# Places of the split weights in on-chip memory: level with the other operand, or 64 bytes beside it

## The chip, the cores and the metric

The kernel runs on one core of a Trainium2 chip. The metric is the device time of one execution in microseconds (us). Before the change the median of three runs is 2192.39 us (2190.46 to 2193.99).

## The reference

One decoder layer on x of 512 tokens by 2048 features, all float32. RMSNorm, a token mixer, an output projection and RMSNorm are added to the residual; then RMSNorm, a gated feed-forward part with a short convolution, and RMSNorm are added again. Cut to what matters here:

```python
h = rmsnorm(x, attn_pre_norm)
proj = h @ w_in                        # 2048 -> 6160 columns
# gated linear attention (4 heads) and differential attention (4 heads)
o = concat([o_a, o_b])                 # 512 x 2048
x = x + rmsnorm(o @ w_o, attn_post_norm)
h = rmsnorm(x, ffn_pre_norm)
up = h @ w_ffn_in                      # 2048 -> 2 x 5632
a, b = up[..., :D_FF], up[..., D_FF:]
a = conv_w[0]*a[t-2] + conv_w[1]*a[t-1] + conv_w[2]*a[t] + conv_b
f = (gelu(a) * b) @ w_ffn_out          # 5632 -> 2048
x = x + rmsnorm(f, ffn_post_norm)
```

## The kernel before, in words

**Splitting.** Every large product is made of three fast ones. A float32 matrix is split into a high part (rounded to the fast type, `F32R`) and a low part (what the rounding lost), and the kernel sums high x high, high x low and low x high. The activations are split once into `ah` and `al` (32 KB each per partition, laid out as 4 token tiles x 16 slices x 128 columns). The weights are split while they stream: `load` brings 128 x 1024 floats ("a granule") into a `raw` tile, and `granule` (lines 103 to 110) lets ScalarE write the high part `whi` (line 107) and VectorE (DVE) the low part `wlo` (line 108) into two tiles with the tag `split`. These come from the pool `wpool`, which has six of them, 4096 bytes each: three granules. A few granules use other pools (`sp1` in the mixer, `sp2` in the passage to the feed-forward part, `sp3` in the down stage), which add a granule or more of room.

**Two shapes of product.** TensorE holds 128 columns of one operand (stationary, loaded by a weight load) and moves columns of the other past it. `mm_n` (lines 157 to 163) holds activations and moves 512 columns of weights; `mm_t` (lines 135 to 145) holds weights and moves 512 columns of activations, or 256 where it is given two token tiles.

**Stages.** 1. The mixer: projections by `mm_n` and `mm_t`, with the attention heads cut into pieces that are run in between. Line 356 and 357 (`forget_gate`) are products with a stationary tile `gas` of 80 columns per step, 16 steps, and 512 moving columns of `ah` and `al`. 2. The output projection, `proj_n` over 4 chunks of 512 columns. For each token tile `evac_m` (lines 601 to 605) takes a finished bank: ScalarE squares it into a scratch tile with a sum, DVE multiplies it by the gain into `m`. 3. `to_ffn`, whose order is written out by hand on all engines: the last chunk, `evac` (the norm's sum, line 629, and its root on GpSimd), `residual` (633), `square` (638), `scale` (644), `turn` (transposes), and between them the first products of the feed-forward part on two token tiles at a time (256 columns). 4. The up stage: units of 512 columns of `w_ffn_in`, ten pairs of units. A unit multiplies 2 x 2 blocks by a scheme of seven products instead of eight; its moving operands are quarters of `ah` and `al` and sums of quarters (`s5`, `s2`, `s3`, `s7`), 256 columns each. `up_prods` (lines 883 to 893) issues for each granule 2 x 4 x 3 = 24 products. GpSimd's queue adds weight blocks to one another by accumulating DMAs (line 840). After each pair of units `token_sums` (lines 949 to 970) makes four sums for the next stage with the helper `add` (line 959 is its operation): `s5`, then `s2` from `s5`, `s7`, and `s3` from `s2`, each stored to memory by a DMA on SP's queue. 5. The down stage, the same scheme with 512 moving columns (lines 988 to 990), and a last group with the final norm.

Outside the stages written by hand a planner orders the instructions of each engine from a model of their times; the order is fixed before the run. Each engine works through its own queue in order. SP's queue issues the loads and stores.

**Places.** A pool gives its tiles out of one stretch of on-chip memory, one after the other, and pools follow each other in the order of the code. `ident` is declared 104 columns wider than used; with it, `ah`, `al` and everything behind it that matters here (`raw`, `split`, the sums of quarters) begin at multiples of 512 bytes. The three lines that make the tiles are:

```python
hi, lo = ((spare or wpool).tile([P, GR], F32R, name=v, tag="split") for v in ("whi", "wlo"))
act(hi, raw, AF.Copy)
tt(lo, raw, hi.bitcast(F32), ALU.subtract)
```

Of the kernel before, what the change touches and what calls it, by code (L numbers as in the profile page):

```python
# [9 lines left out]
F32 = mybir.dt.float32  # L10
F32R = mybir.dt.float32r
U8 = mybir.dt.uint8
AF = mybir.ActivationFunctionType
# [4 lines left out]
P = 128  # L18
# [12 lines left out]
GR = 1024  # L31
# [4 lines left out]
def hybrid_layer(ctx: ExitStack, tc: tile.TileContext, x, attn_pre_norm, w_in, w_alpha_up, b_alpha,  # L36
# [7 lines left out]
    w_f3 = w_ffn_in[0].rearrange("(k p) c -> p k c", p=P)  # L44
    w_y3 = w_ffn_out[0].rearrange("(k p) c -> p k c", p=P)

    def dma(o, i):
        return nc.sync.dma_start(out=o, in_=i)
# [3 lines left out]
    act = nc.scalar.activation  # L52
# [10 lines left out]
    wpool = ctx.enter_context(tc.tile_pool(name="w", bufs=6))  # L63
# [11 lines left out]
    def bank(pool=None):  # L75
        return (pool or psa).tile([P, 512], F32, name="bank", tag="bank")

    fill = []
    pace = [0.0, 0.0]

# [17 lines left out]
    def load(src, a):  # L98
        raw = wpool.tile([P, GR], F32, name="raw", tag="raw", bufs=4)
        dma(raw.rearrange("p (a b) -> p a b", a=a), src)  # L100
        return raw

    def granule(src, a, raw=None, spare=None):
        if raw is None:
            raw = load(src, a)
        hi, lo = ((spare or wpool).tile([P, GR], F32R, name=v, tag="split") for v in ("whi", "wlo"))
        act(hi, raw, AF.Copy)  # L107
        tt(lo, raw, hi.bitcast(F32), ALU.subtract)  # L108
        r = "p (a b) -> p a b"
        return hi.rearrange(r, a=a), lo.rearrange(r, a=a)  # L110

    def rsqrt_mean(ss, n, width=1):
        t = small.tile([P, width], F32, name="ms", tag="ms")
        nc.gpsimd.tensor_scalar(t, ss, 1.0 / n, EPS, ALU.mult, ALU.add)
        r = small.tile([P, width], F32, name="rs", tag="rs")
        nc.gpsimd.tensor_tensor(r, t, nhalf[:, :width], ALU.pow)
        return r
# [5 lines left out]
    def transpose_into_act(src, t, slot0, n):  # L123
        for g in range(0, n, 4):
            m = min(4, n - g)
            b = bank()
            for j in range(m):
                nc.tensor.transpose(b[:, j * P:(j + 1) * P], src[:, (g + j) * P:(g + j + 1) * P], ident)
            bv = b[:, :m * P].rearrange("p (k c) -> p k c", k=m)
            split(ah[:, t, slot0 + g:slot0 + g + m, :], al[:, t, slot0 + g:slot0 + g + m, :], bv)  # L130
# [45 lines left out]

    mixer = ExitStack()
    sp1 = mixer.enter_context(tc.tile_pool(name="sp1", bufs=2))
    mx1 = mixer.enter_context(tc.tile_pool(name="mx1", bufs=1))
    mx = mixer.enter_context(tc.tile_pool(name="mx", bufs=6))  # L180

    def big8(name):
        return mx.tile([P, 2048], F32, name=name, tag="big8", bufs=6)
# [7 lines left out]

    def first_half(c):
        gb = big8("gb")
        jb = mx.tile([P, 1024], F32, name="jb", tag="jb", bufs=1)
        xts = [big8("xt") for _ in range(NT)]
        H2 = [slice(1024 * i, 1024 * (i + 1)) for i in range(2)]
        H4 = [slice(512 * i, 512 * (i + 1)) for i in range(4)]
        rs, raws, w = {}, {}, {}
        banks = [bank(psm) for _ in range(NT)]
        col = C_GV + 512 * c  # L200

        def load_x(t):
            for i in range(2):
                dma(xts[t][:, H2[i]], x2[t * P:(t + 1) * P, H2[i]])

        def load_w(*gs):
            for g in gs:
                raws[g] = load(w_in3[:, 2 * g:2 * g + 2, col:col + 512], 2)

        def weights(g):  # L210
            w[g] = granule(None, 2, raws[g], spare=sp1 if g == 3 else None)

        def square(t):
            ss = small.tile([P, 2], F32, name="ss2", tag="ss2", bufs=4)
            for i in range(2):
                act(jb, xts[t][:, H2[i]], AF.Square, accum_out=ss[:, i:i + 1])
            sm = small.tile([P, 1], F32, name="ss", tag="ss")
            nc.gpsimd.tensor_tensor(sm, ss[:, 0:1], ss[:, 1:2], ALU.add)
            rs[t] = rsqrt_mean(sm, D)

        def scale(t, *ps):
            for i in ps:
                stt(xts[t][:, H4[i]], xts[t][:, H4[i]], rs[t], gb[:, H4[i]], ALU.mult, ALU.mult)

        def turn(t, *ps):
            for i in ps:
                transpose_into_act(xts[t][:, H4[i]], t, 4 * i, 4)

        def prods(t, *gs):
            for g in gs:  # L230
                mm_n(banks, t, g, w[g])

        load_x(0)
        bcast_row(gb[:, H2[0]], attn_pre_norm[0, H2[0]])
        load_w(0, 1, 2)
        load_x(1)
        load_w(3)
        load_x(2)
        load_x(3)
        bcast_row(gb[:, H2[1]], attn_pre_norm[0, H2[1]])  # L240
        square(0)
        scale(0, 0, 1)
        weights(0)
        turn(0, 0, 1)
        weights(1)
        weights(2)
        square(1)
        prods(0, 0, 1)
        scale(1, 0, 1)
        prods(0, 2)  # L250
        weights(3)
        turn(1, 0, 1)
        square(2)
        prods(0, 3)
        square(3)
        scale(2, 0, 1)
        prods(1, 0, 1, 2)
        turn(2, 0, 1)
        prods(1, 3)
        scale(3, 0, 1)  # L260
        prods(2, 0, 1)
        turn(3, 0, 1)
        scale(0, 2, 3)
        prods(2, 2)
        turn(0, 2, 3)
        scale(1, 2, 3)
        prods(2, 3)
        turn(1, 2, 3)
        scale(2, 2, 3)
        prods(3, 0, 1)  # L270
        turn(2, 2, 3)
        scale(3, 2, 3)
        prods(3, 2)
        turn(3, 2, 3)
        prods(3, 3)
        return banks
# [313 lines left out]
    x1d = [dram.tile([P, D], F32, name=f"x1d{t}") for t in range(NT)]  # L590
    wo = ExitStack()
    sp2 = wo.enter_context(tc.tile_pool(name="sp2", bufs=8, reuse_waits="tile"))
    wp = wo.enter_context(tc.tile_pool(name="wo", bufs=1, reuse_waits="tile"))
    m = [wp.tile([P, D], F32, name=f"m{t}") for t in range(NT)]
    g1 = wp.tile([P, D], F32, name="g1")
# [3 lines left out]
    ssm = [wp.tile([P, 4], F32, name=f"ssm{t}") for t in range(NT)]  # L599

    def evac_m(c, t, b):
        jk = wp.tile([P, 512], F32, name="jk5", tag="jk5", bufs=1)
        act(jk, b, AF.Square, accum_out=ssm[t][:, c:c + 1])
        sl = slice(512 * c, 512 * (c + 1))
        tt(m[t][:, sl], b, g1[:, sl], ALU.mult)

    order = [(s + 8) % 16 for s in range(KT)]
    for c in range(3):
# [4 lines left out]
    def to_ffn():  # L613
# [34 lines left out]
                transpose_into_act(xr[t][:, 512 * i:512 * (i + 1)], t, 4 * i, 4)  # L648

        def weights_f(d, c0, g, spare=None):  # L650
            d[g] = granule(w_f3[:, 4 * g:4 * g + 4, c0:c0 + 256], 4, spare=spare)

        for g in range(KT // 2):
            weights(g)
# [69 lines left out]
    fp = fa.enter_context(tc.tile_pool(name="fa", bufs=2, reuse_waits="tile"))  # L724
# [96 lines left out]
    turn = [0]  # L821
    ff = sp3 = None

    class Unit:
        def __init__(self, a, block, prods, chain, out):
            self.a, self.block, self.prods, self.chain, self.out = a, block, prods, chain, out
            self.banks = {}

        def run(self, seg, op, raws):
            c = seg[0]  # L830
            if seg[1] == "0":
                self.banks[c] = self.chain(c)
            for g in range(2):
                turn[0] += 1
                hl = granule(None, self.a, raws[g], spare=sp3 if sp3 and turn[0] % 4 == 0 else None)
                self.prods(self.banks[c], op, g, hl, seg[1] == "0")

        def more(self, raws, j):
# [110 lines left out]
    def token_sums(gi, u0, u1):  # L949
        c, i = (gi - 1) // 2, (gi - 1) % 2  # L950
        T = [slice(0, 256), slice(256, 512)]
        a11, a21, a12, a22 = u0[:, :, T[0]], u0[:, :, T[1]], u1[:, :, T[0]], u1[:, :, T[1]]

        def put(n, src):
            dma(sd[c][n][:, i, :].rearrange("p (n t) -> p n t", n=2), src)

        def add(n, x, y, op):
            t = fp.tile([P, 2, 256], F32, name=n, tag="sum", bufs=3)
            tt(t, x, y, op)
            put(n, t)  # L960
            return t

        put("a11", a11)
        put("a12", a12)
        put("a22", a22)
        s5 = add("s5", a21, a22, ALU.subtract)
        s2 = add("s2", s5, a11, ALU.subtract)
        add("s7", a11, a21, ALU.subtract)
        add("s3", s2, a12, ALU.add)


    place = {"a11": (0, 0), "s5": (1, 0), "s2": (0, 1), "s3": (1, 1), "s7": (2, 0), "a12": (3, 0), "a22": (2, 1)}
# [74 lines left out]
    sp3 = ctx.enter_context(tc.tile_pool(name="sp3", bufs=2, reuse_waits="tile"))  # L1047
# [104 lines left out]
    for q, at in enumerate(((3, 1), (0, 0))):  # L1152
        raw = ff.tile([P, GR], F32, name="st", tag="st", bufs=4)
        dma(raw, ud0[:, 2 * q:2 * q + 2, :].rearrange("p n t -> p (n t)"))
        hi, lo = (piece(v, *at) for v in (ah, al))
# [34 lines left out]
```

## Time and profile before

| what | number |
|---|---|
| median of three runs | 2192.39 us |
| profiled execution | 2189.37 us |
| its span, first to last instruction | 2187.7 us |
| mean granted TensorE clock | 0.996 |
| TensorE busy | 2152.3 us, 98% |
| VectorE busy | 1417.3 us, 65% |
| ScalarE busy | 901.2 us, 41% |
| GpSimd busy | 207.2 us, 9% |
| moved by DMA | 303.83 MB, 139 GB/s on the mean |

Busy times overlap, so they do not add up to the span. PE is TensorE's products, PEld its weight loads, which run beside the products. A row of the costliest groups gives line, engine, operation, out<-in with buffer numbers left out, shape and count, then busy time and the mean duration of one. A matmul's duration is longer than the distance to the next one, since products overlap in the array; distances are read from starts, or from a count in a stretch. A row of the timeline begins with the start and the duration in us. A row for one line gives the least, the median and the greatest duration in ns.

### The profile page before, as it was taken

What the parts mean: (1) busy time and instruction counts of PE and PEld (TensorE: products, weight loads), DVE (VectorE), ACT (ScalarE), POOL (GpSimd) and SP (SyncE); (2) the same over time, 40 slices, a digit from 0 to 9 for tenths busy, and PEclk for the clock granted to TensorE, in tenths of its full rate; (3) what the DMA queues carried; (4) which work ended last, traced back from release to release, by engine and by line L of the source; (5) the groups of instructions that cost most, each with busy time, mean ns of one, the idle gap of its engine ahead of it and who ended that gap; (6) DMA issues with size and microseconds to landing.
All of it is one profiled execution on the core that took longest, in us unless ns stands there. A gap on an engine that the chain in (4) does not pass through costs nothing.

```text
span 2187.7 us, 31874 instructions
## 1 busy us (share of the span) xinstructions
PE 2152.3 (98%) x13009; PEld 1921.1 (88%) x13009; DVE 1417.3 (65%) x1721; ACT 901.2 (41%) x1162; POOL 207.2 (9%) x245
## 2 busy tenths in 40 slices
PE   7999999999999999999999999999999999999997
PEld 6878888888888889899999999999999878888886
DVE  5345554444453246786786776776777777888987
ACT  4233332333342234353443444444444454544433
POOL 1000000000000000011111111011011011011101
PEclk9999999999999999999999999999999999999999
DMA  6322222222224344447657667567567677677663
GB/s 210 103 69 80 74 78 78 77 78 87 77 91 160 106 154 164 115 107 180 153 128 182 145 138 181 139 150 175 135 157 178 169 210 208 183 187 183 158 175 135
DMA packets 218471, 303.83 MB, mean 139 GB/s; under 512 B 11776, under 2 KB 155572, under 8 KB 216404
## 3 DMA queue, kind: packets, MB, share of 16 engines
q1 hardware_dynamic: 165204, 238.87, 32.5%
q0 software_dynamic: 53120, 62.92, 18.5%
q8 instruction: 102, 1.67, 0.3%
q14 instruction: 45, 0.37, 0.1%
HBM read 273.97 MB, written 27.79 MB: 138 GB/s over the span
## 4 chain that ended last, share of the span: by engine, by line
PE 78%; issue 15%; DVE 2%; DMA 2%; POOL 1%; ACT 1%; SPq 0%; POOLq 0%; DVEq 0%; ACTq 0%
PE bank L892 10%; PE bank L891 10%; PE bank L893 10%; PE bank L161 6%; PE bank L163 6%; PE bank L162 6%; PE bank L145 5%; PE bank L143 5%; PE bank L144 5%; PE bank L989 2%; PE bank L990 2%; PE bank L988 2%; PE bank L409 1%; PE bank L477 1%; PE bank L508 1%
## 5 line engine op out<-in xcount | busy, mean ns | idle before, releaser
L108 DVE TENSOR_TENSOR wlo<-raw,whi 128x1024 fp32r<-128x1024 f32 x332 | 404.1, 1221 | 376.8 <-ACT whi L107 366.1
L107 ACT ACTIVATE whi<-raw 128x1024 fp32r<-128x1024 f32 x332 | 350.3, 1059 | 661.7 <-PE bank L892 185.4
L107 ACT ACTIVATE whi<-rt 128x1024 fp32r<-128x1024 f32 x240 | 252.7, 1058 | 306.0 <-PE bank L892 200.3
L108 DVE TENSOR_TENSOR wlo<-rt,whi 128x1024 fp32r<-128x1024 f32 x240 | 292.6, 1221 | 117.4 <-ACT whi L107 113.7
L893 PE MATMUL bank<-ah,wlo 128*128 128x256 f32 x1280 | 362.2, 283 | 0.0
L892 PE MATMUL bank<-al,whi 128*128 128x256 f32 x1280 | 362.2, 283 | 0.0
L891 PE MATMUL bank<-ah,whi 128*128 128x256 f32 x1280 | 362.2, 283 | 0.0
L161 PE MATMUL bank<-whi,ah 128*128 128x512 f32 x640 | 252.7, 398 | 0.2 <-ACT ah L120 0.2
L162 PE MATMUL bank<-wlo,ah 128*128 128x512 f32 x640 | 251.4, 393 | 0.2 <-DVE wlo L108 0.2
L163 PE MATMUL bank<-whi,al 128*128 128x512 f32 x640 | 250.2, 393 | 0.0
L892 PEld LDWEIGHTS bank<-al,whi 128*128 128x128 f32 x1280 | 245.8, 192 | 0.1
L891 PEld LDWEIGHTS bank<-ah,whi 128*128 128x128 f32 x1280 | 245.8, 192 | 0.1
L893 PEld LDWEIGHTS bank<-ah,wlo 128*128 128x128 f32 x1280 | 245.8, 192 | 0.0
L989 PE MATMUL bank<-wlo,ah 128*128 128x512 f32 x560 | 219.8, 393 | 6.6 <-DVE wlo L108 6.6
L990 PE MATMUL bank<-whi,al 128*128 128x512 f32 x560 | 219.2, 392 | 0.0
L988 PE MATMUL bank<-whi,ah 128*128 128x512 f32 x560 | 214.6, 392 | 3.3 <-DVE acc L996 2.0
L143 PE MATMUL bank<-ah,whi 128*128 128x512 f32 (+1 forms) x576 | 214.6, 373 | 0.0
L144 PE MATMUL bank<-al,whi 128*128 128x512 f32 (+1 forms) x576 | 212.9, 370 | 0.0
L145 PE MATMUL bank<-ah,wlo 128*128 128x512 f32 (+1 forms) x576 | 212.5, 369 | 0.3 <-DVE wlo L108 0.3
L163 PEld LDWEIGHTS bank<-whi,al 128*128 128x128 f32 x640 | 120.7, 189 | 26.0 <-DVE al L121 0.3
L162 PEld LDWEIGHTS bank<-wlo,ah 128*128 128x128 f32 x640 | 120.8, 189 | 25.8 <-DVE wlo L108 1.1
L161 PEld LDWEIGHTS bank<-whi,ah 128*128 128x128 f32 x640 | 120.6, 189 | 24.7 <-ACT ah L120 0.6
(222 smaller groups left out, 3716.2 us busy)
## 6 DMA issues: line engine op xcount, KB each, us to landing
raw<-in_w_in_dram SPq DMA_DIRECT2D x96, 512.0 KB, 3.7
raw<-in_w_ffn_in_dram SPq DMA_DIRECT2D x96, 512.0 KB, 4.7
raw<-in_w_ffn_out_dram SPq DMA_DIRECT2D x48, 512.0 KB, 6.7
rt<-in_w_ffn_in_dram SPq DMA_DIRECT2D x40, 512.0 KB, 5.4
rt<-in_w_ffn_in_dram POOLq DMA_DIRECT2D x40, 512.0 KB, 5.9
raw<-in_w_ffn_in_dram POOLq DMA_DIRECT2D x40, 512.0 KB, 7.0
raw<-in_w_o_dram SPq DMA_DIRECT2D x32, 512.0 KB, 3.6
rt<-in_w_ffn_out_dram SPq DMA_DIRECT2D x20, 512.0 KB, 6.3
```

What stands on the lines that cost most here:

```text
L107: act(hi, raw, AF.Copy)
L108: tt(lo, raw, hi.bitcast(F32), ALU.subtract)
L143: mm(o, wh, ah[:, t0:t1, kk, :], start=st, stop=False)
L144: mm(o, wh, al[:, t0:t1, kk, :], start=False, stop=False)
L145: mm(o, wl, ah[:, t0:t1, kk, :], start=False, stop=sp)
L161: mm(banks[t], ah[:, t, s, :], w[0][:, k, :], start=st, stop=False)
L162: mm(banks[t], ah[:, t, s, :], w[1][:, k, :], start=False, stop=False)
L163: mm(banks[t], al[:, t, s, :], w[0][:, k, :], start=False, stop=sp)
L891: mm(o, wh, sh[:, :, kk, :], start=start and kk == 0 and n == 0, stop=False, **NOW)
L892: mm(o, wh, sl[:, :, kk, :], start=False, stop=False, **NOW)
L893: mm(o, wl, sh[:, :, kk, :], start=False, stop=kk == HK - 1, **NOW)
L989: mm(b[j], sh[:, o:o + P], w[1][:, q, :], start=False, stop=False, **NOW)
```

## The change

The split tiles become 1152 instead of 1024 floats long (4608 bytes, 9 x 512), and `granule` uses 1024 of them from an offset: 0 as a rule; 16 floats (64 bytes) or 112 floats (448 bytes, 64 below the next multiple of 512) where its caller gives a place of 64 or -64. `narrow_place` gives -64 and 64 in turns, one for each granule. The up stage's units and the passage's `weights_f` ask for it, the others do not. The pools `sp1` and `sp2` keep tiles of 1024 floats and no offset. To make room, the scratch tile `jb` of the first norm becomes a `big8` tile, `evac_m` squares in place in the bank after the multiplication instead of into a scratch tile before it, and the sums of `token_sums` get two buffers instead of three.

```diff
+    SHIFT = {0: 0, 64: 16, -64: 112}
+    small_pools = []
+    side = [64]
+
+    def narrow_place():
+        side[0] = -side[0]
+        return side[0]
...
-    def granule(src, a, raw=None, spare=None):
+    def granule(src, a, raw=None, spare=None, place=0):
         if raw is None:
             raw = load(src, a)
-        hi, lo = ((spare or wpool).tile([P, GR], F32R, name=v, tag="split") for v in ("whi", "wlo"))
+        if spare in small_pools:
+            hi, lo = (spare.tile([P, GR], F32R, name=v, tag="split") for v in ("whi", "wlo"))
+        else:
+            o = SHIFT[place]
+            hi, lo = ((spare or wpool).tile([P, GR + 128], F32R, name=v, tag="split")[:, o:o + GR]
+                      for v in ("whi", "wlo"))
         act(hi, raw, AF.Copy)
         tt(lo, raw, hi.bitcast(F32), ALU.subtract)
...
     sp1 = mixer.enter_context(tc.tile_pool(name="sp1", bufs=2))
+    small_pools.append(sp1)
...
-        jb = mx.tile([P, 1024], F32, name="jb", tag="jb", bufs=1)
+        jb = big8("jb")[:, :1024]
...
     sp2 = wo.enter_context(tc.tile_pool(name="sp2", bufs=8, reuse_waits="tile"))
+    small_pools.append(sp2)
...
     def evac_m(c, t, b):
-        jk = wp.tile([P, 512], F32, name="jk5", tag="jk5", bufs=1)
-        act(jk, b, AF.Square, accum_out=ssm[t][:, c:c + 1])
         sl = slice(512 * c, 512 * (c + 1))
         tt(m[t][:, sl], b, g1[:, sl], ALU.mult)
+        act(b, b, AF.Square, accum_out=ssm[t][:, c:c + 1])
...
         def weights_f(d, c0, g, spare=None):
-            d[g] = granule(w_f3[:, 4 * g:4 * g + 4, c0:c0 + 256], 4, spare=spare)
+            d[g] = granule(w_f3[:, 4 * g:4 * g + 4, c0:c0 + 256], 4, spare=spare, place=narrow_place())
...
         def __init__(self, a, block, prods, chain, out):
+            self.narrow = prods is up_prods
...
-                hl = granule(None, self.a, raws[g], spare=sp3 if sp3 and turn[0] % 4 == 0 else None)
+                hl = granule(None, self.a, raws[g], spare=sp3 if sp3 and turn[0] % 4 == 0 else None,
+                             place=narrow_place() if self.narrow else 0)
...
         def add(n, x, y, op):
-            t = fp.tile([P, 2, 256], F32, name=n, tag="sum", bufs=3)
+            t = fp.tile([P, 2, 256], F32, name=n, tag="sum", bufs=2)
             tt(t, x, y, op)
```

## The prediction

> **What bounds the kernel now.** I read the page's busy times and costliest groups first, then the stretches, then who waits for whom in the longest stage, then single lines and rows.
>
> ```profile
> PE 2152.3 (98%) x13009; PEld 1921.1 (88%) x13009; DVE 1417.3 (65%) x1721; ACT 901.2 (41%) x1162; POOL 207.2 (9%) x245
> ```
> ```profile
> 720.00:800.00 80.00, 80.00 (x354) 66.24 (x354) 27.12 (x26) 24.04 (x34) 0.00 (x0) 1.00 0.31 107
> 930.00:1090.00 160.00, 160.00 (x1335) 160.00 (x1334) 117.48 (x118) 75.11 (x82) 20.51 (x16) 1.00 0.62 145
> ```
> ```profile
> ACT whi L107 <- PE bank L892: 384.4, 248, 2.1
> DVE u L919 <- PE bank L893: 18.3, 20, 0.9
> ```
>
> The stretch 930 to 1090 us lies in the up stage of the feed-forward part (line 891 to 893, 256 columns move). TensorE takes all of it, at granted clock 1.00, and 160.00 us / 1335 = 119.9 ns: one product starts each 120 ns. The second fence is the list of waits from 930 to 1725 us. No wait of TensorE is in it; ScalarE waits 384.4 us in 248 pieces for TensorE to free a split tile. DVE is busy 117.48 / 160 = 73%, the DMA engines 62%. So the pace of this stage is the distance between two products and nothing else. Where 512 columns move (720 to 800 us), the distance is 80.00 / 354 = 226 ns, with TensorE again full.
>
> ```profile
> L891 PEld LDWEIGHTS bank<-ah,whi x1280: 187/192/192, 927.1 to 1738.7; 128*128 128x128 f32 x183
> L891 PE MATMUL bank<-ah,whi x1280: 277/283/283, 927.3 to 1738.8; 128*128 128x256 f32 x183
> L891 PE MATMUL bank<-s5h,whi x320: 283/283/283, 933.0 to 1704.5; 128*128 128x256 f32 x160
> L891 PE MATMUL bank<-s2h,whi x320: 283/283/283, 936.2 to 1710.3; 128*128 128x256 f32 x160
> L891 PE MATMUL bank<-s3h,whi x320: 283/283/283, 941.9 to 1716.3; 128*128 128x256 f32 x160
> ```
>
> Line 891 issues 1280 + 3 x 320 = 2240 products, the stage 3 x 2240 = 6720. The distance hardly varies: median and longest product are both 283 ns, median and longest weight load both 192 ns. Here a load runs beside every product for its whole length: 128 columns against 256. That is the stage the change aims at.
>
> **The change, part by part.** First, the places. By the declared sizes, ah, al, the sums and all split tiles begin at multiples of 512 bytes now, and a slice of 128 columns is 512 bytes: stationary and moving slice are always level. After it, granules with place 0 are level as before (the tiles are 4608 = 9 x 512 bytes apart), and those of the up stage sit 64 bytes above or below. No instruction is added; 6720 products are touched, and of the 384 of `to_ffn` that move 256 columns those of the four granules out of `wpool` (wa 0 to 2, wb 3): 4 x 48 = 192. Together 6912. One nanosecond in the distance is 6.9 us, 0.32% of the time.
>
> How much is in it? Two kinds of rows bound it. The first are products at the edge of the rhythm:
>
> ```profile
> 927.29 0.28 PE L891 MATMUL bank<-ah,whi 128*128 128x256 f32 x1
> 927.40 0.28 PE L892 MATMUL bank<-al,whi 128*128 128x256 f32 x1
> 927.52 0.28 PE L893 MATMUL bank<-ah,wlo 128*128 128x256 f32 x1
> ```
> ```profile
> 838.16 0.28 PE L144 MATMUL bank<-al,whi 128*128 128x256 f32 x1
> ...
> 839.11 0.28 PE L143 MATMUL bank<-ah,whi 128*128 128x256 f32 x1
> ```
>
> Right behind a 512-column product two distances take 0.23 us: 115 ns each. After a break, eight take 0.95 us: 119 ns each, and then the rhythm is back at 120. Operands, sizes and places are the same; only how load and product lie in time to each other differs. So 120 ns is no floor. The fastest product of line 891 took 277 ns against 283, its load 187 against 192: some 6 ns are there to be won, and the lower end is 120 - 6 = 114 ns.
>
> The second are the only products of this type whose operands are not level in a fixed way. The weights of `forget_gate` have 80 columns, 320 bytes a step, while ah goes on by 512: the relation moves by 64 bytes (modulo 256) at each step of two products, and is back after four steps.
>
> ```profile
> 123.94 0.40 PE L356 MATMUL bank<-ah,gas 128*80 128x512 f32 x1
> 124.18 0.39 PE L357 MATMUL bank<-al,gas 128*80 128x512 f32 x1
> 124.41 0.39 PE L356 MATMUL bank<-ah,gas 128*80 128x512 f32 x1
> ...
> 124.86 0.39 PE L356 MATMUL bank<-ah,gas 128*80 128x512 f32 x1
> ...
> 125.78 0.40 PE L356 MATMUL bank<-ah,gas 128*80 128x512 f32 x1
> ...
> 131.28 0.39 PE L161 MATMUL bank<-whi,ah 128*128 128x512 f32 x1
> ```
>
> 32 products take 131.28 - 123.94 = 7.34 us, 229.4 ns each against the level 227 (226 to 227 by the stretch above). The eight of one cycle take 125.78 - 123.94 = 1.84 us, 230. So the place does change the distance, and it does so in steps of 64 bytes with a period of 256; on the mean over the four relations, and at 512 columns, it costs 2.4 ns. That is the upper end for 256 columns: 122.4 ns. A mean over four, two of which are the change's, can't say which of the four is dear.
>
> Between 114 and 122.4 I take 116.5: nearer the rows of the very same instruction (115, 119) than those of another shape, and between these two. My reason is a guess from these rows: at level a load and a product that start together are also in the same 64 bytes together, each time, and a shift takes just that away. 6912 x (116.5 - 120) = -24.2 us. TensorE is the limit throughout, so it all counts; at 116.5 DVE is busy 73% x 120 / 116.5 = 76%.
>
> The Trainium skill speaks against this: "TensorE: Matmul & The Clock Gate", under what happens when a matmul is issued, gives TensorE two independent read ports, so that loading the next weights takes no read bandwidth from the running product. By it the shift would change nothing. The distances of lines 356 and 357, which differ with the place alone, do not agree with it; nothing here shows that place matters at 256 columns.
>
> Second, `evac_m`. ScalarE's square now writes into the bank that DVE reads for the gain, so it waits for DVE; before, both ran side by side. In chunks 0 to 2 twelve such pairs lie under 18 products (18 x 227 ns = 4.1 us) before the bank is needed again. For tile 3 it is exposed:
>
> ```profile
> 835.27 0.68 DVE L605 TENSOR_TENSOR m<-bank,g 128x512 f32<-128x512 f32 x1
> 835.87 0.14 DVE L629 TENSOR_REDUCE ss<-ssm 128x1 f32<-128x4 f32 x1
> 835.93 1.21 DVE L108 TENSOR_TENSOR wlo<-raw,whi 128x1024 fp32r<-128x1024 f32 x1
> 837.86 2.35 DVE L633 SCALAR_TENSOR_TENSOR m<-m,rs,xr 128x2048 f32<-128x2048 f32 x1 [0.72 <-POOL rs L116]
> ```
> ```profile
> 833.68 0.60 ACT L603 ACTIVATE jk<-bank 128x512 f32<-128x512 f32 x1 [2.43 <-PE bank L163]
> 834.17 0.19 ACT L603 ACTIVATION_READ_ACCUMULATOR jk<-bank 128x1 f32 x1
> 834.27 1.06 ACT L107 ACTIVATE whi<-raw 128x1024 fp32r<-128x1024 f32 x1
> ```
> ```profile
> 844.52 0.39 PE L145 MATMUL bank<-ah,wlo 128*128 128x256 f32 x1 [0.33 <-DVE wlo L108]
> ```
>
> The square was done at 834.4, under DVE's earlier work. Now it runs from 835.95 to 836.7, and the split behind it on ScalarE ends at 837.8 instead of 835.3. The reduction, and behind it on DVE the low part, come 0.8 to 1.9 us later; so do residual, square and the next split, for which TensorE already waits at 844.52. Ends 0.8 and 1.9; I take 1.1, from the DVE chain: +1.1 us.
>
> Third, two `sum` buffers instead of three: s7 waits for the store of s5, s3 for that of s2 (it overwrites its own operand).
>
> ```profile
> 1745.91 0.69 DVE L959 TENSOR_TENSOR s<-u 128x512 f32<-128x512 f32 x1
> 1746.63 0.69 DVE L959 TENSOR_TENSOR s<-s,u 128x512 f32<-128x512 f32 x1
> 1747.24 0.68 DVE L959 TENSOR_TENSOR s<-u 128x512 f32<-128x512 f32 x1
> 1748.70 0.69 DVE L959 TENSOR_TENSOR s<-s,u 128x512 f32<-128x512 f32 x1 [0.78 <-DMA sd4s<-s]
> 1749.31 1.22 DVE L108 TENSOR_TENSOR wlo<-rt,whi 128x1024 fp32r<-128x1024 f32 x1
> ```
> ```profile
> DMA to landing us min/median/max: 2.0/2.8/6.9
> ```
> ```profile
> 1750.59 0.51 PE L989 MATMUL bank<-wlo,ah 128*128 128x512 f32 x1 [3.75 <-DVE wlo L108]
> ```
>
> In nine of the ten calls the split tiles that stand ready (ScalarE's waits for TensorE) cover it: 0. In the last, nothing does: s7 goes to 1748.7, s3 behind the store of s2 to about 1750.1, and the low part at 1749.31, for which TensorE stands, comes 1.4 us later (ends: 0, where s2's store lands in 2.0 us, and 2.8): +1.4 us. The squares' scratch `jb` becomes one of six `big8` buffers, the sixth, which stood unused: 0.
>
> The sum: -24.2 + 1.1 + 1.4 = -21.7. The profiled execution took 2189.4 us (span 2187.7 and 1.7 around it), so 2167.7; the median of the runs lies 3.0 above that execution: **2171 us**.
>
> **The rivals.** *No effect of the place*: the distance stays at 120.0, only the two small losses remain: 2192.4 + 2.5 = 2194.9. For it: the even 283 ns in four groups whose moving tiles lie far apart. Against it: the 115 ns. The Trainium skill's two read ports, named above, would make this the result.
>
> *The shift costs* (the other side): load and product meet in the middle of the stream instead of at its head. Place: every product of the up stage. Price by lines 356 and 357: +2.4 ns, 6912 x 2.4 = +16.6, with the small losses 2211. It decides from a distance of 120.3 on: 6912 x 0.3 = 2.1, with the small losses 0.2% of the time. For it: level is the best of what 512 columns show. Against it: there the load needs half the product's time, here all of it.
>
> *DVE gives it back*: with a faster TensorE the nine covered calls of `token_sums` stop DVE long enough to empty the split tiles. Price: 2.8 us of a store less the 0.8 already waited, 2.0 in each of ten calls, +20: 2191. Against it: 24% of DVE is idle there.
>
> **How the numbers follow.** Forecast (114 to 118.5 ns) 0.62, no effect 0.14, the shift costs 0.18, DVE gives it back 0.06. About 0.2% (4.4 us) is what a measurement can tell from no change: faster 0.62, same 0.14 + 0.06 = 0.20, slower 0.18. The forecast's own range is 6912 x (114 - 120) = -41.5, 2153, to 118.5, 2185. The range 2150 to 2200 holds that, no effect, DVE, and the nearer part of the shift that costs (up to +0.7 ns).
>
> **What would show it.** In 160 us of the up stage some 1373 products instead of 1335; the medians of lines 891 to 893 below 283 ns and their loads near 187; ScalarE still waiting for TensorE; 226 ns unchanged where 512 columns move. Two different distances in alternating granules would say that above and below are not alike. Medians of 283 with 120 ns are no effect; above 283, the shift costs. TensorE waiting for `wlo` within the stage is DVE. The gap before 844.5 should grow by about 1 us, that before 1750.6 by 1.4. I am wrong if the distance falls while the time does not, or if the 512-column stages move.

## The result, and the profile after

The changed kernel takes 2153.78 us (median, 2150.73 to 2159.61) against 2192.48 before: ratio 0.9827, 95% interval 0.9805 to 0.985. The forecast was 2171, inside a range of 2150 to 2200. The gain is 38.7 us where 21.4 were forecast.

The busy times on the page of the changed kernel, whose lines stand 13 to 16 further down (line 891 is now 907, 107 is 120, 143 is 156):

```profile
PE 2110.2 (98%) x13009; PEld 1878.9 (87%) x13009; DVE 1415.0 (66%) x1721; ACT 899.1 (42%) x1162; POOL 206.7 (10%) x245
```

A stretch of its up stage (length; then busy time and instructions of TensorE, its weight loads, DVE, ScalarE and GpSimd; granted clock, share of the DMA engines, GB/s), and the products of line 907 (least, median and greatest duration in ns):

```profile
1000.00:1160.00 160.00, 160.00 (x1414) 160.00 (x1413) 122.90 (x125) 76.51 (x83) 23.11 (x18) 1.00 0.70 164
```
```profile
L907 PEld LDWEIGHTS bank<-ah,whi x1280: 187/188/192, 931.4 to 1699.5; 128*128 128x128 f32 x183
L907 PE MATMUL bank<-ah,whi x1280: 276/276/281, 931.6 to 1699.6; 128*128 128x256 f32 x183
L907 PE MATMUL bank<-s2h,whi x320: 276/276/281, 940.1 to 1672.2; 128*128 128x256 f32 x160
```

160.00 us hold 1414 products instead of 1335: one each 113.2 ns (starts, read one by one, are 113, 113 and 114 ns apart, 113.3). The median product went from 283 to 276 ns, its load from 192 to 188. TensorE is still the limit, but with less in hand: from 932 to 1695 us ScalarE waits 287.6 us for a split tile to come free, against 384.4, and waits for weights have grown (on ScalarE from 32.3 us to 49.5; GpSimd had none before). First the line before, then those of the changed kernel:

```profile
ACT whi L107 <- DMA raw<-in_w_ffn_in_dram: 32.3, 11, 3.9
```
```profile
ACT whi L120 <- PE bank L908: 287.6, 205, 4.4
POOL rt L856 <- DMA raw<-in_w_ffn_in_dram: 75.2, 6, 13.2
ACT whi L120 <- DMA raw<-in_w_ffn_in_dram: 49.5, 18, 4.8
```

Where 512 columns move, nothing changed: 355 products start in 720 to 800 us, 354 before.

```profile
720.00:800.00 80.00, 80.00 (x355) 66.26 (x354) 26.31 (x26) 23.87 (x34) 0.00 (x0) 1.00 0.31 106
```

Cut at the starts of products, the two profiled executions compare as follows; each number is the distance between two starts in the traces, in us.

| stretch | before | after | difference |
|---|---|---|---|
| first product to the passage (`to_ffn`, 256 columns) | 823.8 | 824.7 | +0.9 |
| passage | 50.32 | 53.55 | +3.2 |
| passage to the up stage | 43.55 | 43.55 | 0.0 |
| up stage, to the start of its last segment | 806.1 | 762.8 | -43.3 |
| from there to the last product | 441.4 | 442.0 | +0.6 |

So the up stage won more than forecast, and the passage lost more.

The changed up stage has two rhythms, not one. The first, the third, the seventh and the ninth granule of the stage, 24 products each (the counts take in three products that began before):

```profile
931.84:934.66 2.82, 2.82 (x27) 2.82 (x25) 2.59 (x3) 1.79 (x2) 0.00 (x0) 1.00 1.19 232
937.40:940.12 2.72, 2.72 (x27) 2.72 (x26) 2.72 (x3) 1.91 (x3) 0.00 (x0) 1.00 0.00 0
948.65:951.47 2.82, 2.82 (x27) 2.82 (x26) 2.39 (x3) 1.22 (x2) 1.25 (x1) 1.00 0.84 115
954.21:956.93 2.72, 2.72 (x27) 2.72 (x26) 1.86 (x2) 0.90 (x1) 0.00 (x0) 1.00 1.14 285
```

All four lie 64 bytes below. The first and the seventh take 2.82 / 24 = 117.5 ns a product (117.8 between the starts inside), the third and the ninth 113.3. Both rhythms hold by themselves: the slow one ended when the second granule came, from below to above; a break in the sixth (two distances of 287 and 221 ns) brought it back; it stayed through the step from above to below, and ended again at the next step up. That is why the experiments ask first whether the turns are needed.

### The profile page after: what moved, and what is told of

Its sections match the earlier page's. It is cut to its first block, busy times and chain, and to the rows that moved or that the text cites. A ratio compares the mean times of both kernels' runs of the same rounds, so it can differ in the third digit from the quotient of the medians.

```text
span 2149.0 us, 31874 instructions
## 1 busy us (share of the span) xinstructions
PE 2110.2 (98%) x13009; PEld 1878.9 (87%) x13009; DVE 1415.0 (66%) x1721; ACT 899.1 (42%) x1162; POOL 206.7 (10%) x245
## 4 chain that ended last, share of the span: by engine, by line
PE 39%; issue 16%; DVE 3%; DMA 2%; POOL 1%; ACT 1%; POOLq 0%; DVEq 0%; ACTq 0%
PE bank L908 7%; PE bank L909 7%; PE bank L907 7%; PE bank L1004 5%; PE bank L1005 4%; PE bank L1006 4%; PE bank L158 1%; PE bank L156 1%; PE bank L157 1%; DMA raw<-in_w_ffn_in_dram 1%; DVE wlo L121 1%; POOL rt L856 1%; DMA rt<-in_w_ffn_out_dram 1%; POOL raw L856 1%; DVE acc L1144 0%
## 5 line engine op out<-in xcount | busy, mean ns | idle before, releaser
L909 PE MATMUL bank<-ah,wlo 128*128 128x256 f32 x1280 | 353.6, 276 | 0.2 <-DVE wlo L121 0.2
L908 PE MATMUL bank<-al,whi 128*128 128x256 f32 x1280 | 353.4, 276 | 0.0
L907 PE MATMUL bank<-ah,whi 128*128 128x256 f32 x1280 | 353.3, 276 | 0.0
L909 PEld LDWEIGHTS bank<-ah,wlo 128*128 128x128 f32 x1280 | 240.3, 188 | 0.4 <-DVE wlo L121 0.4
L908 PEld LDWEIGHTS bank<-al,whi 128*128 128x128 f32 x1280 | 240.3, 188 | 0.1
L907 PEld LDWEIGHTS bank<-ah,whi 128*128 128x128 f32 x1280 | 240.3, 188 | 0.1
```

The lines of the kernel that those rows point to most:

```text
L907: mm(o, wh, sh[:, :, kk, :], start=start and kk == 0 and n == 0, stop=False, **NOW)
L908: mm(o, wh, sl[:, :, kk, :], start=False, stop=False, **NOW)
L909: mm(o, wl, sh[:, :, kk, :], start=False, stop=kk == HK - 1, **NOW)
```

## The experiments

**Every place level (`e1_level`).**

```diff
     def narrow_place():
-        side[0] = -side[0]
-        return side[0]
+        return 0
```

> The changed kernel with every place 0: tiles, buffers and evac_m as changed, all split tiles level. If the place alone brings the gain: distance 120.0 ns in the up stage, the stage 806 us as before, and the time above before by what the other edits cost, by the ledger of the two traces 5 to 6 us: 2197 to 2199. If the other layout (tiles 4608 bytes apart) or another edit brings it: distance near 113.5 and a time near 2154.

Measured: 2196.52 us, ratio 1.0025 (1.0014 to 1.0036). The up stage takes 806.1 us, as before:

```profile
1000.00:1160.00 160.00, 160.00 (x1335) 160.00 (x1335) 118.25 (x120) 73.17 (x80) 20.55 (x16) 1.00 0.65 154
```

The place alone brings the gain; tiles 4608 bytes apart, the other buffers and `evac_m` bring none. They cost 0.25%, 5.2 us by the medians.

**One side only (`e2_above`, `e3_below`).** The same function returns 64 always, or -64 always.

> Every shifted granule 64 bytes above, none below. If a shift is all that counts: 113.3 ns after each break, the same time as the changed kernel within 2 us. If the turns are what brings the rhythm back after a break (in the changed kernel two granules ran at 117.8 until the place next went from below to above): 117.8 ns from the first break on for long stretches, up to 6720 x 4.4 = 30 us longer, 2184 at most.

> Every shifted granule 64 bytes below. If above and below are alike: as the run with all above, whichever that is. If only the step from below to above sets the fast rhythm, this one stays at 117.8 ns throughout: 2180 to 2184. A mere shift that counts: 2154.

Measured: 2182.15 us (0.9958, 0.9943 to 0.9973) and 2180.22 us (0.9953, 0.9938 to 0.9967). The same stretch, first all above, then all below:

```profile
1000.00:1160.00 160.00, 160.00 (x1361) 160.00 (x1360) 119.20 (x121) 74.24 (x81) 21.36 (x17) 1.00 0.65 157
```
```profile
1000.00:1160.00 160.00, 160.00 (x1361) 160.00 (x1360) 118.77 (x121) 74.81 (x81) 21.84 (x17) 1.00 0.65 155
```

1361 products, 117.6 ns by this count and 117.8 by starts, from the first granule to the end of the stage, on either side. Above and below are alike, and a shift that never turns takes 2.2 of the 6.7 ns here. In the changed kernel the other two thirds come with the turns.

**One step (`e8_one_step`).** All above, but for the 40th granule of the stage.

```diff
+        side[0] += 1
+        return -64 if side[0] == 64 + 8 + 40 else 64
```

> All granules 64 bytes above, but for the 40th of the up stage, which is 64 below. If one step from below to above sets the rhythm and it then holds: 117.8 ns up to granule 40, 113.3 from granule 41 to the next break, stage near 766 us. If the turns have to go on: 113.3 in a few granules about the 40th at most, stage near 791 us.

Measured once: 2159.53 us. The 39 granules ahead of the step, and 99 behind it, from the 42nd on:

```profile
932.33:1042.57 110.24, 110.24 (x938) 110.24 (x937) 84.04 (x83) 51.54 (x55) 12.97 (x11) 1.00 0.63 148
1048.12:1317.40 269.28, 269.28 (x2379) 269.28 (x2378) 208.28 (x213) 130.31 (x143) 35.99 (x28) 1.00 0.68 159
```

110.24 us / 936 = 117.8 ns ahead of it, 269.28 / 2376 = 113.3 behind it. One step sets the fast rhythm, and it then holds by itself, later through two breaks (granules 152 and 160); a third, in granule 264, put the slow one back, and with no further step it stayed to the end. The stage took 768.6 us. The turns repair what breaks undo.

**All offsets (`e4_scan`).** Eight granules at each offset (in floats), in the up stage and, by the same list, in the down stage.

```diff
+    SCAN = [0, 4, 8, 12, 16, 20, 24, 28, 32, 36, 40, 44, 48, 52, 56, 60,
+            16, 48, 0, 32, 8, 40, 24, 56, 4, 36, 20, 52, 12, 44, 28, 60, 64, 80, 96]
-            o = SHIFT[place]
+            o = place
```

> One look: offsets of 0 to 240 bytes in steps of 16, eight granules each, in rising and then in another order, then 256, 320 and 384, in the up stage; the same 16 offsets in the down stage, where 512 columns move and the split tile is the moving operand. If what counts is which 64 bytes of 256 the two slices are in: 120 ns at 0 and 256, one or two plateaus of 113 to 118 elsewhere, 320 as 64 and 384 as 128. If any offset frees them, all but 0 and 256 are alike. In the down stage 227 ns at 0 and up to 236 elsewhere, as lines 356 and 357 had it; less than 226 anywhere would mean that level is not the best place there.

Measured once, 2187.96 us. Seven of the 35 blocks of 192 products, at 0, 32, 64, 128, 192, 256 and 320 bytes:

```profile
933.02:956.05 23.03, 23.03 (x195) 23.03 (x194) 20.41 (x19) 10.93 (x12) 2.55 (x2) 1.00 0.46 85
978.77:1001.49 22.72, 22.72 (x195) 22.72 (x194) 17.63 (x19) 11.24 (x13) 2.56 (x2) 1.00 0.51 116
1024.10:1045.87 21.77, 21.77 (x195) 21.77 (x194) 15.07 (x17) 9.05 (x10) 4.00 (x4) 1.00 0.78 199
1114.24:1137.02 22.78, 22.78 (x195) 22.78 (x194) 15.50 (x16) 11.97 (x14) 2.56 (x2) 1.00 0.84 206
1205.45:1227.21 21.76, 21.76 (x195) 21.76 (x194) 20.66 (x23) 14.00 (x17) 2.29 (x2) 1.00 0.43 92
...
1657.40:1680.42 23.02, 23.02 (x195) 23.02 (x194) 15.15 (x17) 9.01 (x10) 4.16 (x4) 1.00 0.76 190
1680.42:1703.04 22.62, 22.62 (x195) 22.62 (x194) 21.20 (x24) 15.09 (x18) 2.27 (x2) 1.00 0.46 111
```

Divided by 192: 119.9, 118.3, 113.4, 118.6, 113.3, 119.9, 117.8 ns. All offsets, from the starts in the trace (ns; two numbers where the two visits differ):

| bytes | 0 | 16 | 32 | 48 | 64 | 80 | 96 | 112 | 128 | 144 | 160 | 176 | 192 | 208 | 224 | 240 |
|---|---|---|---|---|---|---|---|---|---|---|---|---|---|---|---|---|
| ns | 120 | 118.3 | 118.3 | 117.8 | 113.3 | 118.8 | 117.4 | 120 | 118.6 | 118.3, 120 | 120 | 118.1 | 113.3 | 116.7 | 116.7 | 120 |

256 gives 120 like 0, and 384 in its first six granules 118.6 like 128 (its last two, which follow on 512-column products, ran at 120.0), as a period of 256 bytes would have it. There is no plateau: the fast rhythm is at 64 and at 192 alone, 16 bytes beside them it is gone. 320, which by that period lies as 64 does, ran at 117.8, the distance of 64 in `e2_above`; it had been entered from level, while 64 was entered from 48 and from 240, 192 from 176 and from 64. So at these two places the rhythm seems to depend on where one comes from; elsewhere the two visits differ at 144 alone.

In the down stage, where the split tile is the moving operand of 512 columns, four blocks of 96 products at 48, 96, 192 and 240 bytes:

```profile
1807.24:1829.32 22.08, 22.08 (x98) 18.02 (x97) 18.40 (x18) 13.62 (x16) 2.41 (x2) 1.00 0.80 235
1873.86:1896.27 22.41, 22.41 (x98) 18.02 (x97) 19.60 (x22) 11.89 (x12) 3.58 (x3) 1.00 1.03 267
2007.83:2030.23 22.40, 22.40 (x98) 17.95 (x97) 20.59 (x22) 10.38 (x11) 2.38 (x2) 1.00 0.50 124
2075.15:2096.93 21.78, 21.78 (x98) 18.02 (x97) 16.54 (x19) 9.44 (x10) 2.38 (x2) 1.00 0.55 133
```

230.0, 233.4, 233.3 and 226.9 ns against 226.7 level. None of the 16 is under level: where 512 columns move the change rightly leaves the tiles there.

**Both operands shifted (`e5_both`).** All weights above, and the tiles of s5, s2 and s3 begin 64 bytes later too.

> All weights 64 bytes above, and the sums of quarters s5, s2 and s3, moving operands of three of the seven products, 64 bytes above too; the quarters in ah and al stay. If the relation of the two operands counts: 120 ns for the products of s5, s2 and s3, which are level again, and 117.8 (or 113.3) for those of ah and al. If the weights' own place counts: one distance for all.

Measured once: 2172.32 us. A granule of ah, one of s5, one of s2, one of ah:

```profile
1051.98:1054.70 2.72, 2.72 (x26) 2.72 (x25) 2.45 (x3) 1.02 (x2) 0.00 (x0) 1.00 0.19 65
1057.56:1060.44 2.88, 2.88 (x26) 2.88 (x25) 2.88 (x5) 1.07 (x3) 0.00 (x0) 1.00 0.00 0
1060.44:1063.32 2.88, 2.88 (x26) 2.88 (x25) 2.88 (x4) 2.26 (x4) 0.00 (x0) 1.00 0.00 0
1080.14:1082.87 2.73, 2.73 (x26) 2.73 (x26) 1.22 (x1) 1.07 (x2) 1.30 (x2) 1.00 0.28 35
```

2.88 / 24 = 120.0 ns where both are shifted, 113.3 where only one is. The relation of the two operands counts, not the place of the weights. Each of the 20 returns from the level sums to ah went into the fast rhythm within a few products, though at 320 bytes the way from level led into the slow one, and so did, in this run as in `e2_above`, the way from the level 512-column products into the first granule.

**evac_m alone (`e7_evac`), two sum buffers alone (`e10_sums`).** Each is one hunk of the change, on the kernel before.

> The kernel before with evac_m alone as changed (all places level, distance 120). If it costs what the passage lost in the changed kernel: passage 53 to 55 us instead of 50.3, with TensorE at half its clock for some products in it, and 2195 to 2197. By the predicted term alone: +1.1, 2192.5.

> The kernel before with two sum buffers instead of three. By the predicted term the up stage stays at 806.1 us and the low part behind the last four sums comes 1.4 us later (0 to 2.8): 2192 to 2195. If the nine earlier calls are not covered: breaks in the up stage, up to 20 us.

`e7_evac`: 2195.43 us, ratio 1.0015 (1.0006 to 1.0024), 3.3 us; its passage takes 54.1 us instead of 50.3. The hunk turns an order round. Before, square and gain of a bank did not run side by side: in each of the sixteen pairs the gain began after the square's end. First a pair of the kernel before, then the same one in `e7_evac`, where the square begins after the gain's end and the norm's sum waits for it:

```profile
822.38 0.60 ACT L603 ACTIVATE jk<-bank 128x512 f32<-128x512 f32 x1 [4.27 <-PE bank L163]
823.10 0.69 DVE L605 TENSOR_TENSOR m<-bank,g 128x512 f32<-128x512 f32 x1 [1.30 <-ACT jk L603]
```
```profile
823.67 0.68 DVE L603 TENSOR_TENSOR m<-bank,g 128x512 f32<-128x512 f32 x1
824.45 0.58 ACT L604 ACTIVATE bank<-bank 128x512 f32<-128x512 f32 x1 [4.38 <-DVE m L603]
825.17 0.16 DVE L628 TENSOR_REDUCE ss<-ssm 128x1 f32<-128x4 f32 x1 [0.81 <-ACT bank L604]
```

ScalarE, which had been early, now stands behind DVE's earlier work. What TensorE sees of it, shown on the changed kernel, its rows and then a stretch:

```profile
844.42 0.28 PE L158 MATMUL bank<-ah,wlo 128*128 128x256 f32 x1
846.63 0.38 PE L156 MATMUL bank<-ah,whi 128*128 128x256 f32 x1 [1.94 <-ACT whi L120]
846.85 0.28 PE L157 MATMUL bank<-al,whi 128*128 128x256 f32 x1
847.89 0.39 PE L158 MATMUL bank<-ah,wlo 128*128 128x256 f32 x1 [0.76 <-DVE wlo L121]
...
849.79 0.41 PE L158 MATMUL bank<-ah,wlo 128*128 128x256 f32 x1
850.00 0.41 PE L156 MATMUL bank<-ah,whi 128*128 128x256 f32 x1
850.22 0.41 PE L157 MATMUL bank<-al,whi 128*128 128x256 f32 x1
```
```profile
846.80:851.40 4.60, 3.84 (x19) 3.64 (x20) 4.60 (x6) 0.72 (x1) 0.00 (x0) 0.64 0.37 118
```

TensorE stands twice, for a high and for a low part, and then its products are 0.21 us apart for some 3.4 us: it was granted half its clock. The Trainium skill ("TensorE: Matmul & The Clock Gate", Part 1) tells of a gate that watches windows of 3.4 us and halves the clock after an idle one; the 3.4 us at half the clock agree. An idle window of that length is not in the rows: ahead of the half clock stand two gaps of 2.2 and 1.0 us between starts, with two products between them. The same gaps do not always bring it: see `e11_after`.

`e10_sums`: 2193.18 us, ratio 1.0011 (1.0002 to 1.0021), 2.4 us; no break in the nine earlier calls. The last four sums in it:

```profile
1746.56 0.68 DVE L959 TENSOR_TENSOR s<-u 128x512 f32<-128x512 f32 x1
1747.28 0.69 DVE L959 TENSOR_TENSOR s<-s,u 128x512 f32<-128x512 f32 x1
1749.33 0.69 DVE L959 TENSOR_TENSOR s<-u 128x512 f32<-128x512 f32 x1 [1.36 <-DMA sd4s<-s]
1752.13 0.69 DVE L959 TENSOR_TENSOR s<-s,u 128x512 f32<-128x512 f32 x1 [2.10 <-DMA sd4s<-s]
1752.74 1.22 DVE L108 TENSOR_TENSOR wlo<-rt,whi 128x1024 fp32r<-128x1024 f32 x1
```

Before, the low part came 3.40 us after the first of the sums (1749.31 - 1745.91); here 6.18 (1752.74 - 1746.56): 2.8 later. The two costs add to 0.26%, and `e1_level` has 0.25%.

**Room made otherwise (`e6_narrow_pad`).** As the period is 256 bytes, 64 floats of padding do; what they save pays for `evac_m` and the sums as before the change.

```diff
-    SHIFT = {0: 0, 64: 16, -64: 112}
+    SHIFT = {0: 0, 64: 16, -64: 48}
-            hi, lo = ((spare or wpool).tile([P, GR + 128], F32R, ...
+            hi, lo = ((spare or wpool).tile([P, GR + 64], F32R, ...
```

> The changed kernel with tiles of 1088 floats and offsets of 16 and 48 (64 above, and 192 bytes, which is 64 below a multiple of 256); the room pays for evac_m in its old order and for three sum buffers. If only the place modulo 256 bytes counts: 113.3 ns, up stage 763 us. If the serial evac_m costs the 4 us that the passage lost: the passage back at some 49 us, the end of the up stage as it was before, and 2148 to 2150 in all. If the passage lost them to the layout: 2153 as the changed kernel.

Measured: 2150.97 us, ratio 0.982 (0.9805 to 0.9834), 1 us above the expected stretch. The up stage takes 763.6 us, the passage 49.8, no half clock in it. So 192 bytes do what 448 did.

**A turn in every triple (`e9_hi_lo`, timed again as `e12_hi_lo_timed`).** On top of that, the high part lies above and the low part below in each shifted granule.

```diff
+            hi, lo = ((spare or wpool).tile([P, GR + 64], F32R, name=v, tag="split")[:, o:o + GR]
+                      for v, o in (("whi", SHIFT[abs(place)]), ("wlo", SHIFT[-abs(place)])))
```

> Tiles of 1088 floats, evac_m and sums as before the change; in every shifted granule the high part lies 64 bytes above and the low part 64 below, so that the relation turns within each triple of products. If any step between below and above may set the fast rhythm: 113.3 ns at once after each break, no granule at 117.8. If a step itself costs something: a distance above 113.3 throughout; the first triples after a step in the changed kernel (116, 122, 119) would say about 118.

> The same kernel as the run with high parts above and low parts below, now timed. If its one look (2147.9) was typical: 2146 to 2150, ratio near 0.980. If that was a good draw: 2150 to 2152, as the run with the narrow pad.

The first run took 2147.9; timed, 2148.82 us, ratio 0.9812 (0.9798 to 0.9825). Its first granule of the up stage, which ran at 117.8 in the changed kernel:

```profile
927.52:930.26 2.74, 2.74 (x26) 2.74 (x25) 2.41 (x3) 1.94 (x2) 0.00 (x0) 1.00 1.19 212
```

2.74 / 24 = 114.2 ns, with four slow products at the start, and 113.3 from there on; no granule sits at 117.8. Constant steps cost nothing in the distance. The stage took 764.6 and 766.1 us in the two traces all the same, for it has more breaks than in the changed kernel (762.8); in the second trace TensorE's products waited 1.8 us for low parts, against 0.2.

**The changed kernel again (`e11_after`).**

> The changed kernel once more, beside the other runs of this call: 2151 to 2156, breaks in the up stage that hold a granule or two at 117.8 ns each, passage with a stretch at half the clock.

2152.98 us, ratio 0.9829 (0.9814 to 0.9845). The expectation missed the half clock. The passage has the same two waits as above, to a hundredth of a us, but TensorE kept its full clock behind them, and the passage took 52.0 us instead of 53.6:

```profile
845.98 0.38 PE L156 MATMUL bank<-ah,whi 128*128 128x256 f32 x1 [1.94 <-ACT whi L120]
846.20 0.28 PE L157 MATMUL bank<-al,whi 128*128 128x256 f32 x1
847.24 0.39 PE L158 MATMUL bank<-ah,wlo 128*128 128x256 f32 x1 [0.76 <-DVE wlo L121]
```
```profile
846.10:850.70 4.60, 3.84 (x31) 3.64 (x32) 4.60 (x6) 0.87 (x2) 0.00 (x0) 1.00 0.36 114
```

Of the nine traces with the changed `evac_m` six have a half clock in the passage, which then takes 53.6 to 55.3 us; three have none (`e2_above`, `e3_below`, this one), at 51.8 to 52.3. With `evac_m` as before the passage takes 49.5 to 50.3. So the waits cost about 2 us each time, and the clock some 1.5 on top in some executions only. In the up stage the break in granule 6 led back to the fast rhythm at once this time; granules 1 and 279 ran at 117.8.

The medians of `e6_narrow_pad` and `e12_hi_lo_timed` are 2.8 and 5.0 us under the 2153.78 of the changed kernel, but their intervals overlap with its own. They were not timed side by side; that they beat it is likely and not shown.

## Why the prediction was right, and where not

1. *The up stage is paced by the distance of products and by nothing else.* Right: the stage followed it in each run, 806.1 us at 120, 791.3 at 117.8, 762.8 at 113.3.

2. *120 ns is no floor; 114 is the lower end.* Right in kind. The end came from the fastest product (277 ns against 283); measured are 276 and 113.3, just beyond it.

3. *116.5 ns.* This is the term that was mis-sized. I put it between the rows at the edge of the rhythm (115 and 119), as if the change would land somewhere in between. It landed on the end: 6912 x (113.3 - 120) = -46.3 us instead of -24.2. The rows held the hint: eight products at 119 on the way back to 120 showed that a rhythm settles, and a settled one need not be a mean. Read one by one in the trace, the two distances that made up the 115 are 113 and 119 ns.

4. *The reason, that at level load and product are in the same 64 bytes together.* It fell. By it all places out of the same 64 bytes would be alike; but 128 bytes gives 118.6 and 208 gives 116.7, and at 64 itself both 113.3 and 117.8 hold. The forecast had the right sign for a reason that is not the right one; that was luck. So was the part of the turns: the forecast gave them no effect, but without them (`e2_above`, `e3_below`) the distance is 117.8, which makes 6912 x (117.8 - 120) = -15.2 us, and the times are only 9 and 11 us shorter than before.

5. *122.4 as the upper end, from lines 356 and 357.* Those rows told of 512 columns and were right there: 230 to 233 ns at three of the shifted places shown. They say nothing of 256, where no block of the scan was over 120.0.

6. *The rule of two independent read ports* (the Trainium skill, "TensorE: Matmul & The Clock Gate", Part 2) would have meant no effect of the place. `e1_level` against the changed kernel shows 6.7 ns of it. What in the chip makes it is not shown by any run.

7. *evac_m, +1.1.* Mis-sized: 3.3 us timed, 3.8 in the passage of the trace, some 1.5 of it the half clock. Square and gain had not run side by side before, as I had it; the change turned their order round. For tile 3 the chain was the right one, but the residual on DVE was queued behind the low part, and that behind the split on ScalarE, which I had put 1.9 late and then not taken. Tile 2, for which I had put nothing, was exposed as well: behind it DVE reached the gain of tile 3 3.2 us after the start of the passage, before 1.9. And I had not seen that the longer gaps could halve the clock behind them.

8. *Two sum buffers, +1.4.* The upper end, 2.8, was right for the low part; 2.4 us timed. The nine covered calls were covered.

The sum with measured terms is -46.3 + 3.3 + 2.4 = -40.6; the medians give -38.7. The rest is breaks and granules at 117.8 (the trace has 1, 7, 279 and most of 6, some 4 x 24 x 4.5 ns = 0.4 us), and the end of the kernel, which varies: from the last segment of the up stage to the last product it took 439 to 447 us in the traces with a level down stage, 442.0 and 445.6 in the two of the changed kernel.

The rival that DVE would give the gain back did not come: within the stage TensorE's products wait 0.2 us for a low part, and its loads 0.6. But it came nearer: ScalarE's wait for TensorE in the stage fell by a quarter, and waits for weights took its place.

## What to carry to other kernels

Where one product follows another for hundreds of microseconds, look at the distance between starts, not at busy time, and try the relative place of stationary and moving operand in steps of 64 bytes over 256: here it was worth 5.4% of the stage. Read the distance by granule, not on the mean, since a rhythm can settle in more than one state and a break decides in which; a small step of the place, repeated, brings it back. Count what the room for such a shift costs elsewhere: here a turned order cost some 2 us of waits in a stage written by hand, and in some executions 1.5 us more, because the clock went down behind them.

## What the runs showed that was not expected

Two products of one kind, with the same operands in the same relation, run at 113.3 or at 117.8 ns, and either state holds for hundreds of products. Which one is taken depends on the way in: the step from below to above led to the fast one in each case in these traces, and breaks led to either. The way in from the level 512-column products led to the slow one in each kernel that shifts the high and low part of a granule alike; the way in from level 256-column products led to the slow one at 320 bytes and to the fast one, 20 times over, in `e5_both`. What decides there stays open; so does why 64 and 192 bytes are the two places out of sixteen.
